# Reordering the products of a Strassen–Winograd step where a new token half enters the down projection (decoder block, eight cores)

## The chip, the cores and the metric

The kernel runs on one Trainium2 chip, on all 8 cores of it, one batch element per core. The metric is the device time in microseconds (us) of the slowest core. Most executions agree within 0.3%, but a program on eight cores also has a slower state, in which the cores of one die run at a lower granted clock.

## The reference, cut to what matters

A decoder block in two parts: token mixing (attention and mLSTM head groups), then a gated MLP with a causal three-tap convolution. The change touches the last line alone, the multiplication by `w_down`, and how the kernel passes into it.

```python
D_MODEL = 2048; BATCH = 8; SEQ = 2048; D_FF = 5632; FFN_CONV = 3
...
        h2 = _rmsnorm(x, norm_ffn_g[layer]).astype(x.dtype)
        u = _causal_dwconv(h2 @ w_up[layer], ffn_conv_w[layer], ffn_conv_b[layer])
        gate, val = jnp.split(u, 2, axis=-1)
        x = x + (jax.nn.silu(gate) * val) @ w_down[layer]
```

## The kernel before

Both MLP multiplications use the Winograd form of Strassen's method: seven products of half blocks in place of eight, paid for with sums of activations and of weights on the vector engine. The down stage has 16 steps, called d0 to d15: eight groups of output columns for the first 1024 tokens, then the same eight for the second 1024. A step computes four tiles of the output (x11, x12, x21, x22: token quarter, column block), from

- activations A11, A12, A21, A22 (token quarter, inner half). The up stage writes them to DRAM (`actd`); for d0, and again for d8, they are read back in eight loads of 1280 KB. S1 = A21 + A22, S2 = S1 − A11, S3 = A11 − A21, S4 = A12 − S2 are made on the vector engine in halves of 5120 elements;
- weights B11, B12, B21, B22 (640 KB each, loaded new for each step by the pool queue, as bf16) and T1 = B12 − B11, T2 = B22 − T1, T3 = B22 − B12 (written over B12), T4 = B21 − T2;
- a remainder: 20 of 22 chunk pairs of the inner dimension go through Winograd, the last two through "plain" products with their own small tiles of activations (`pA`) and weights (`pB`).

The products are P1 = A11·B11, P2 = A12·B21, P3 = S4·B22, P4 = A22·T4, P5 = S1·T1, P6 = S2·T2, P7 = S3·T3, each of 20 matmuls (128x128 by 128x512); with 16 plain ones a step has 156. They accumulate in PSUM banks; `acc` adds a bank to a tile of the residual `x1`, and the last one stores the tile to `outT`. Activation loads, `x1` loads and output stores share the sync queue.

Which tiles a product and a sum need, and how a step's weights get loaded (cut; every `...` is a cut):

```python
        def load(self, nm):
            k = ("B11", "B12", "B21", "B22").index(nm)
            i = self.q[nm]
            K.dma(pool, qv[i], w_down[self.g, :, k * KQ * 128:(k + 1) * KQ * 128], B_q[i], True)
...
        def t_sum(self, which):
            q = self.q
            o_, a, b = {1: ("T1", "B12", "B11"), 2: ("T2", "B22", "T1"), 3: ("B12", "B22", "B12"),
                        4: ("T4", "B21", "T2")}[which]
            tt_op(qv[q[o_]], B_q[q[o_]], qv[q[a]], B_q[q[a]], qv[q[b]], B_q[q[b]], ALU.subtract)
...
        def P1(self):
            self.p(self.s, "A11", "B11", True)
        def P5(self):
            self.p(2 + self.s, "S1", "T1", True)
        def P6(self):
            self.p(self.s, "S2", "T2", False)
        def P2(self):
            self.p(4 + self.s, "A12", "B21", True)
        def P7(self):
            self.p(self.s, "S3", "B12", False)
        def P4(self):
            self.p(self.s, "A22", "T4", False)
        def P3(self):
            self.p(2 + self.s, "S4", "B22", False)
```

What follows a product in program order: the load of the next step's tile into the buffer just read.

```python
    def aft(d, k):
        nx = downs[d + 1] if d + 1 < ND else None
        ...
        sw = nx.pr != downs[d].pr
        if sw:
            if k in (1, 5, 6, 2):
                a_load(*{1: ("A11", 1, "A11"), 5: ("S1", 1, "A12"), 6: ("S2", 1, "A21"), 2: ("A12", 1, "A22")}[k])
        elif k in (1, 5, 6, 2):
            nx.load({1: "B11", 5: "B12", 6: "B22", 2: "B21"}[k])
            if k == 2:
                nx.load_p()
        if k in (5, 2, 7, 4):
            nx.xload({5: "x11", 2: "x22", 7: "x12", 4: "x21"}[k])
```

The last up step's weight loads, and d0 (`gl` is the last up step, `g` is d0):

```python
        if n == len(ups) - 1:
            for i, nm in ((4, "B21"), (2, None), (3, "B22")):
                q_make(i)
                if nm:
                    d0.load(nm)
            d0.t_sum(1)
...
    a_make("A22")
    a_load("A22", 0, "A22")
    gl.P4()
    gl.taps(0)
    gl.P3()
    ...
    g.P1()
    acc(g, "x11", "A")
    aft(0, 1)
    g.P2()
    a_sum("S1", "A21", "A22", ALU.add)
    d0.t_sum(2)
    a_sum("S2", "S1", "A11", ALU.subtract)
    g.P5()
    d0.t_sum(3)
    d0.t_sum(4)
    a_sum("A21", "A11", "A21", ALU.subtract)
    acc(g, "x22", "B")
    g.P6()
    ...
    g.P7()
    ...
    plain_load(0)
    ...
    g.P4()
    g.P3()
    downs[1].t_sum(1)
    for nm, b in (("x12", "B"), ("x11", "C"), ("x21", "A"), ("x22", "D")):
        g.plain(nm)
        acc(g, nm, b, True)
    aft(0, 7)
    aft(0, 4)
    for k in (2, 3, 4):
        downs[1].t_sum(k)
```

The softmax here doesn't subtract the row's maximum and nothing guards it: scores larger than these inputs give would overflow.

## Time and profile before

| quantity | before |
|---|---|
| time, median of the first 3 runs | 2900.98 us (2900.79 to 2904.68) |
| span of the profiled run's slowest core (core 1) | 2902.3 us |
| spans of its eight cores | 2886.4 to 2902.3 us |
| tensor engine busy, core 1 | 97% |
| time lost in the down stage, mean of cores / core 1 | 47.1 / 51.9 us |

The last row is the measure called the **excess**. On each core it is the time from the start of the last up step's P4 (the first matmul after a gap of 0.84 us) to the end of the last matmul, less 2512 matmuls at 0.2158 us, 542.1 us. It counts waits and half clock together; half clock means stretches in which the tensor engine is granted 0.50 of its clock. In a timeline line the columns are start, length, engine, source line, operation, number of instructions, and in brackets the idle time just before and what ended it; L1262 is the down stage's matmuls, L1055 every bf16 sum, L1448 (L1450 after the change) the accumulations into `x1`, and L1286 and L1290 belong to the up stage.

### The profile page before, as it was taken

Reading aid. Unit: us, or ns where it says so; the run is one execution under the profiler, and the core shown is the slowest. Engines: PE = TensorE matmul, PEld = TensorE weight load, DVE = VectorE, ACT = ScalarE, POOL = GpSimd, SP = SyncE. Lnnn points to the kernel's source line nnn. Section 1 sums busy time; section 2 is a strip of 40 time slices with the busy share of each in tenths; the row PEclk is TensorE's granted clock in tenths of the full one; section 3 lists DMA queues with packets and bytes.
Section 4 is the critical chain, followed back from the end, with each engine's and each line's share of the span. In section 5 each row is a group of like instructions: output and inputs, shape, how many; then the busy total and the mean of one; then the engine's idle time right before and its main releaser. Section 6 shows DMA issues by size and latency. Waiting matters only on the chain.

```text
span 2902.3 us, 44182 instructions; the slowest of 8 cores (2886.4 to 2902.3 us)
## 1 busy us (share of the span) xinstructions
PE 2805.5 (97%) x14698; PEld 1333.3 (46%) x14698; DVE 1801.4 (62%) x2409; ACT 1222.3 (42%) x2013; POOL 369.1 (13%) x535
## 2 busy tenths in 40 slices
PE   6999999999999999999999999999999979997999
PEld 3444554555555544444444444444444434443444
DVE  4664543777777646688877777777788753324332
ACT  3567654666666521145555555555555400000000
POOL 0000001333333200011100000000011100000000
PEclk9999999999999999999999999999999989998999
DMA  8352455434444695757733333333368867787774
GB/s 201 94 82 51 78 113 119 92 85 88 90 88 87 132 250 179 181 87 105 106 66 66 66 66 66 66 66 66 66 99 148 206 140 152 145 220 151 144 150 93
DMA packets 223230, 330.23 MB, mean 114 GB/s; under 512 B 27008, under 2 KB 144192, under 8 KB 220960
## 3 DMA queue, kind: packets, MB, share of 16 engines
q0 software_dynamic: 98064, 156.79, 36.5%
q1 hardware_dynamic: 124944, 170.63, 20.2%
q8 instruction: 121, 1.98, 0.3%
q14 instruction: 101, 0.83, 0.1%
HBM read 386.30 MB, written 71.20 MB: 158 GB/s over the span
## 4 chain that ended last, share of the span: by engine, by line
PE 83%; DMA 6%; DVE 5%; issue 3%; ACT 2%; DVEq 0%; SPq 0%; POOL 0%; ACTq 0%; POOLq 0%
PE ps L1262 52%; PE ps L812 10%; PE ps L562 6%; PE ps L1136 4%; PE ps L433 3%; DMA mem<-xA 2%; DMA mem<-actd 2%; PE ps L911 2%; PE ps L913 1%; PE ps L898 1%; PE ps L421 1%; PE ps L836 1%; DVE mem L403 1%; DMA outT<-mem 1%; DVE mem L1055 1%
## 5 line engine op out<-in xcount | busy, mean ns | idle before, releaser
L1262 PE MATMUL ps<-mem 128*128 128x512 bf16 x7424 | 1617.2, 381 | 48.2 <-DMA mem<-actd 21.6
L1262 PEld LDWEIGHTS ps<-mem 128*128 128x128 bf16 x7424 | 727.9, 98 | 937.8 <-issue 72.7
L1320 DVE SCALAR_TENSOR_TENSOR mem<-mem,cfs 128x1024 f32<-128x1024 f32 x352 | 452.2, 1285 | 240.1 <-ACT mem L1314 154.6
L812 PE MATMUL ps<-mem 128*128 128x512 bf16 x1536 | 381.5, 379 | 0.0
L1055 DVE TENSOR_TENSOR mem<-mem 128x1024 bf16<-128x1024 bf16 (+3 forms) x324 | 308.6, 979 | 74.9 <-DMA mem<-w_down 58.3
L1448 DVE TENSOR_TENSOR mem<-ps,mem 128x512 f32<-128x512 f32 x128 | 88.2, 691 | 299.3 <-PE ps L1262 295.1
L166 POOL DMA_DIRECT2D mem<-w_up x240 | 126.9, 530 | 1145.3 <-PE ps L1262 744.7
L562 PE MATMUL ps<-mem 128*128 128x512 bf16 x1024 | 229.9, 380 | 0.0
L1136 PE MATMUL ps<-mem 128*128 128x512 bf16 x1024 | 224.9, 381 | 4.3 <-DMA mem<-mixd 3.5
L1286 ACT ACTIVATE mem<-ps 128x512 f32<-128x512 f32 x176 | 105.0, 597 | 288.8 <-PE ps L1262 288.6
L1314 ACT ACTIVATE mem<-mem,cfs 128x1024 f32<-128x1024 f32 x176 | 216.9, 1232 | 17.5 <-DVE mem L1290 10.7
L812 PEld LDWEIGHTS ps<-mem 128*128 128x128 bf16 x1536 | 148.6, 98 | 156.2 <-issue 8.0
L823 DVE SCALAR_TENSOR_TENSOR mem<-ps,cfs,mem 128x512 bf16<-128x512 f32 x192 | 143.9, 750 | 53.4 <-ACT mem L821 39.9
L1136 PEld LDWEIGHTS ps<-mem 128*128 128x128 bf16 x1024 | 100.3, 98 | 125.7 <-issue 8.2
L900 ACT ACTIVATE mem<-ps 128x512 bf16<-128x512 f32 x216 | 126.0, 583 | 70.8 <-PE ps L898 61.7
L832 POOL TENSOR_TENSOR mem<-mem 128x512 f32<-128x512 f32 x96 | 111.1, 1158 | 320.2 <-DMA mem<-mem 237.4
L901 DVE TENSOR_TENSOR mem<-mem 128x512 bf16<-128x512 bf16 x216 | 104.4, 484 | 75.7 <-ACT mem L900 75.3
L562 PEld LDWEIGHTS ps<-mem 128*128 128x128 bf16 x1024 | 99.1, 98 | 112.3 <-issue 1.4
L1290 DVE TENSOR_TENSOR mem<-ps,mem 128x512 f32<-128x512 f32 x176 | 120.4, 684 | 0.8 <-ACT mem L1286 0.7
L1159 ACT ACTIVATE mem<-mem 128x512 f32<-128x512 f32 x64 | 40.2, 629 | 169.7 <-DVE mem L1154 169.7
L433 PE MATMUL ps<-mem 128*128 128x512 bf16 x512 | 111.5, 379 | 0.0
L166 POOL DMA_DIRECT2D mem<-w_down x75 | 39.6, 531 | 535.0 <-PE ps L1262 434.2
(127 smaller groups left out, 2351.9 us busy)
## 6 DMA issues: line engine op xcount, KB each, us to landing
mem<-w_up POOLq DMA_DIRECT2D x240, 256.0 KB, 5.4
mem<-w_down POOLq DMA_DIRECT2D x60, 640.0 KB, 8.9
actd<-mem SPq DMA_DIRECT2D x88, 256.0 KB, 4.4
mem<-actd SPq DMA_DIRECT2D x16, 1280.0 KB, 13.0
mem<-xA SPq DMA_DIRECT2D x32, 512.0 KB, 10.7
mem<-xA SPq DMA_DIRECT2D x64, 256.0 KB, 6.1
x1d<-mem SPq DMA_DIRECT2D x64, 256.0 KB, 5.4
mem<-x1d SPq DMA_DIRECT2D x64, 256.0 KB, 5.3
```

Source lines behind the costliest of these rows:

```text
L166: eng.e.dma_start(out=o_, in_=i_).then_inc(sb.dsem, 16)
L433: bk, B_bk = dense(5, [lambda e, b, kc=kc: e.matmul(b[:], sl[:, kc, hm * 128:(hm + 1) * 128], hT[:, kc, tsl], start=(kc == 0), stop=(kc == ...
L562: ins = pe.e.matmul(ps[bi][:], *lr(kc), start=(kc == 0), stop=(kc == KC - 1))
L812: ins = pe.e.matmul(bank[:], sl[:, kc, c0:c0 + 128], hT[:, kc, tsl], start=(kc == 0), stop=(kc == KC - 1))
L823: K.op(dve, lambda e: e.scalar_tensor_tensor(out=sc[nm], in0=bank[:], scalar=cf[:, gcol:gcol + 1], in1=tab[:, tsl], op0=ALU.mult, op1=ALU. ...
L900: K.op(act, lambda e: e.activation(out=pt[:, c0:TT], in_=Sb[:, c0:TT], func=AF.Exp), [B_S], [B_p])
L1055: K.op(dve, lambda e: e.tensor_tensor(out=out, in0=a, in1=b, op=op), [B_a, B_b], [B_out])
L1136: ins = pe.e.matmul(ps[bi][:], wo_v[jb][:, kc, (jc % 4) * 128:(jc % 4 + 1) * 128], mix(T, kc), start=(kc == 0), stop=(kc == KC - 1))
L1262: K.mm([lambda e, l=l, r=r, s_=(first and i == 0): e.matmul(ps[bi][:], l, r, start=s_, stop=False, skip_group_check=True) for i, (l, r) in ...
L1290: K.op(dve, lambda e: e.tensor_tensor(out=y, in0=ps[bank][:], in1=snap[si], op=ALU.add), [B_ps[bank], B_snap[si]], [self.B_y[gv]])
L1314: K.op(act, lambda e: e.activation(out=self.a[gv], in_=self.y[gv][:, 2:1026], func=AF.Identity, scale=self.wc(gv, 2), bias=cf[:, CF_FCB + ...
L1320: K.op(dve, lambda e, k=k: e.scalar_tensor_tensor(out=self.a[gv], in0=self.y[gv][:, k:k + 1024], scalar=self.wc(gv, k), in1=self.a[gv], op ...
```

## The change

The intent: at d0 and d8, run products for which the data are there early, so that the tensor engine need not wait for the last activations and the sums made of them. P7 (which needs S3 = A11 − A21 alone) and P4 (which takes A22 as it comes) move ahead of P5 and P6, with banks of their own. For that S3 gets its own tile and is made in the up stage; T4, and with it T2, come earlier, so B22 is loaded before B21; the first half of A22 is loaded after the last up P6; each quarter of the plain activations gets a buffer record of its own, so their loads no longer wait for each other. The core of the diff (buffer addresses, the bodies of loads by halves and the d8 sums cut):

```diff
-    d_q = [dict(B11=1, B12=0, B22=3, B21=4, T1=2, T2=5, T4=2, spare=7)]
+    d_q = [dict(B11=1, B12=0, B22=4, B21=3, T1=2, T2=5, T4=1, spare=7)]
...
-        def P7(self):
-            self.p(self.s, "S3", "B12", False)
+        def P7(self, own=None):
+            self.p(self.s if own is None else own, "S3", "B12", own is not None)
...
+        if n == len(ups) - 1:
+            q_make(4)
+            d0.load("B22")
+            a_make("S3", [0])
+            a_sum("S3", "A11", "A21", ALU.subtract, [0])
...
         g.P6()
+        if n == len(ups) - 1:
+            a_make("A22", [0])
+            a_load("A22", 0, "A22", [0])
...
         if n == len(ups) - 1:
-            for i, nm in ((4, "B21"), (2, None), (3, "B22")):
-                q_make(i)
-                if nm:
-                    d0.load(nm)
+            q_make(3)
+            d0.load("B21")
+            q_make(2)
             d0.t_sum(1)
+            a_make("S3", [1])
+            a_sum("S3", "A11", "A21", ALU.subtract, [1])
...
     gl.P4()
-    gl.taps(0)
+    a_make("A22", [1])
+    a_load("A22", 0, "A22", [1])
     gl.P3()
...
-    g.P1()
-    acc(g, "x11", "A")
-    aft(0, 1)
-    g.P2()
-    a_sum("S1", "A21", "A22", ALU.add)
-    d0.t_sum(2)
-    a_sum("S2", "S1", "A11", ALU.subtract)
-    g.P5()
...
+    d0.t_sum(2)
+    g.P1()
+    d0.t_sum(4)
+    a_sum("A21", "A21", "A22", ALU.add)
+    acc(g, "x11", "A")
+    g.P2()
+    g.P7(7)
+    a_sum("S2", "A21", "A11", ALU.subtract)
+    g.P4(1)
...
+    aft(0, 1)
+    aft(0, 5)
+    g.P5()
+    acc(g, "x22", "B")
+    aft(0, 2)
+    a_make("S4")
+    a_sum("S4", "A12", "S2", ALU.subtract)
+    g.P6()
+    mid(g)
+    aft(0, 6)
     g.P3()
     downs[1].t_sum(1)
-    for nm, b in (("x12", "B"), ("x11", "C"), ("x21", "A"), ("x22", "D")):
-        g.plain(nm)
-        acc(g, nm, b, True)
+    plains(g)
     aft(0, 7)
     aft(0, 4)
     for k in (2, 3, 4):
         downs[1].t_sum(k)
...
         if d == NG:
+            a_sum("S4", "A11", "S2", ALU.subtract)
+            acc(g, "x11", "A")
+            aft(d, 1)
             g.P2()
-            ...
+            aft(d, 2)
+            ...
+            g.P7(7)
+            ...
+            g.P4(1)
             g.P5()
             acc(g, "x22", "B")
             aft(d, 5)
+            ...
             g.P6()
+            mid(g)
             aft(d, 6)
             g.P3()
+            nx.t_sum(1)
+            plains(g)
```

## The prediction

> **What bounds the kernel now.** I read the page's engine shares and slices first, then who the tensor engine waits for, then its timeline around the two dips that the slices show, and last the vector engine and the DMA queues in those two stretches.
>
> ```profile
> PE 2805.5 (97%) x14698; PEld 1333.3 (46%) x14698; DVE 1801.4 (62%) x2409; ACT 1222.3 (42%) x2013; POOL 369.1 (13%) x535
> ...
> PE   6999999999999999999999999999999979997999
> ...
> DVE  4664543777777646688877777777788753324332
> ...
> PEclk9999999999999999999999999999999989998999
> ```
>
> The matmul stream is the bound: 97% busy. A slice is 72.6 us, and in the down stage only slices 33 and 37 fall to 7: the start of each half of the down stage, where the activations of a new token half come in (call its steps d0 and d8; there are 16 steps, d0 to d15, of 7 x 20 + 16 = 156 matmuls). What those two cost, on the slowest core, by waits and then in order of time:
>
> ```profile
> PE ps L1262 <- DMA mem<-actd: 21.6, 3, 16.8
> ...
> PE ps L1262 <- DVE mem L1055: 11.0, 6, 4.4
> PE ps L1262 <- DVE mem L1448: 7.9, 2, 7.0
> ```
>
> ```profile
> 2303.61 12.25 PE L1262 MATMUL ps<-mem 128*128 128x512 bf16 x56 [0.84 <-ACT mem L1286]
> 2318.34 2.32 PE L1262 MATMUL ps<-mem 128*128 128x512 bf16 x10 [2.49 <-DVE mem L1055]
> 2325.07 9.39 PE L1262 MATMUL ps<-mem 128*128 128x512 bf16 x30 [4.40 <-DVE mem L1055]
> 2341.41 5.91 PE L1262 MATMUL ps<-mem 128*128 128x512 bf16 x20 [6.95 <-DVE mem L1448]
> ...
> 2360.19 2.42 PE L1262 MATMUL ps<-mem 128*128 128x512 bf16 x8 [3.13 <-DMA mem<-actd]
> ...
> 2613.99 2.32 PE L1262 MATMUL ps<-mem 128*128 128x512 bf16 x10 [1.60 <-DVE mem L1055]
> ...
> 2642.61 254.96 PE L1262 MATMUL ps<-mem 128*128 128x512 bf16 x1168 [16.84 <-DMA mem<-actd]
> ```
>
> At d0 the third product needs S1, which needs the last quarter of the activations (A22), loaded only after the last up product; then the vector engine makes every other sum in one run of eight, and an accumulation queued behind them frees the bank for the next product (the 6.95 us):
>
> ```profile
> 2315.37 2.83 DVE L1055 TENSOR_TENSOR mem<-mem 128x5120 bf16<-128x5120 bf16 x1 [2.96 <-DMA mem<-actd]
> 2322.09 17.97 DVE L1055 TENSOR_TENSOR mem<-mem 128x5120 bf16<-128x5120 bf16 x8 [3.90 <-DMA mem<-actd]
> 2339.99 1.28 DVE L1448 TENSOR_TENSOR mem<-ps,mem 128x512 f32<-128x512 f32 x2
> ```
>
> At d8 the big wait is for the small "plain" activations, the last 2 of 22 chunk pairs. The sync queue issues them late, and one after the other:
>
> ```profile
> SPq L60 <- DMA outT<-mem: 46.5, 17, 21.1
> SPq L60 <- DMA mem<-actd: 31.5, 4, 15.1
> ```
>
> The clock pays once more after the long wait, which the timeline books as busy time (columns after the stretch: its length, busy time of PE, PEld, DVE, ACT, POOL, granted clock, DMA):
>
> ```profile
> 2642.60:2645.00 2.40, 2.40 (x6) 0.85 (x7) 0.07 (x1) 0.00 (x0) 0.00 (x0) 0.50 0.31 80
> 2645.00:2650.00 5.00, 5.00 (x17) 1.92 (x16) 0.62 (x1) 0.00 (x0) 0.00 (x0) 0.69 0.69 227
> ```
>
> **The loss in numbers.** A warm product of 8 matmuls takes 1.727 us (an up step of 7 is 12.085 us apart from the next), so one matmul costs 0.2158 us. From the end of the 0.84 us gap to the end are 2 x 8 + 16 x 156 = 2512 matmuls, 542.1 us. Core 1 takes from 2303.61 to 2642.61 + 254.96 = 2897.57, 593.96 us: 51.9 us too long. The waits in the timeline explain 40.5 of them, half clock after them the rest: step d1 begins at 2367.9 (its third accumulation at 2376.87 less 0.3 and two products of 4.32), so d0 lost 27 us; d9 begins at 2661.8, so d8 lost 24.5. The same sum for cores 0 to 7 gives 45.3, 51.9, 44.8, 49.3, 44.3, 45.8, 48.7 and 46.8 us. This is the ceiling of the change. Core 2 enters the stage last (2304.58, core 1 at 2303.61), so it may end last when both lose alike.
>
> **What the Trainium skill says.** "TensorE: Matmul & The Clock Gate", Part 1: the array falls to half clock after an idle window of some 3.4 us and needs about as long a busy one to come back; warm N=512 matmuls start every 215.7 ns. The trace agrees: 0.50 then 0.69 after the 16.84 us wait, and 215.8 ns. So gaps over 3.4 us cost more than themselves, and small ones do not. "VectorE: DVE Perf Modes", Side-by-side: a 16-bit tensor_tensor makes two elements a cycle, plus about 150 cycles; for 5120 that is an estimate of 2.83 us, and the trace has 2.82; so these sums get no cheaper and the change can only reorder them. "DMA: Bandwidth & Descriptors", Queues, rings and completion order: each DMA engine takes turns between queues, and starts a queue's own transfers in order. The trace fits: three output stores issued at 2597.8 behind eight activation loads landed after 22.3 us (2.9 is their median); a weight load that shared the engines with A22 took 12.8 us, alone 7.0 to 8.8. "SBUF — State Buffer", Who interferes with whom: tensor_tensor has no two-port mode, so a busy vector engine should not starve the pool queue's descriptor writing. No long bf16 run in this trace tests that.
>
> **The change, part by part.** The matmuls stay the same in kind and number. In d0 and d8 the products go P1 P2 P7 P4 P5 P6 P3 in place of P1 P2 P5 P6 first. P7 needs only S3 (A11 - A21), P4 only A22 as it comes. Both get own banks, 7 and 1, so nothing in a bank has to be read out before them; for that bank 0 and bank 7 are added by 5 accumulations in place of 2: 3 more per step, 6 x 0.69 = 4.1 us of vector time. S3 gets its own tile and is made while the up stage still runs. Half of A22 loads after the last P6 (about 2299), not after the last P7 (2306); the other half after P4. B22 now comes before B21. The plain tiles get one buffer per half, so their loads no longer wait for each other.
>
> *d0, vector engine as the clock of it.* From the last but one up step, with 2.75 us for a half sum (back to back), 1.43 for a weight sum, 0.6 for an accumulation, 2.6 for two taps: S3 first half 2299.5 to 2302.3, taps 2304.9, up sum 2305.5, product 2306.6, T1 2308.1, S3 second half 2310.8, up sum 2311.4, T3 2312.9, four taps 2318.1, product 2319.2, T2 2320.7, T4 2322.1, S1 2327.6, accumulation 2328.2, S2 2333.7, accumulation 2334.3, S4 2339.8, five accumulations 2343.1, next T1 2344.5, accumulation 2345.2. The tensor engine: P3 of the last up step starts 0.4 late, P1 to 2311.9, P2 2316.2, P7 2320.5 (S3 and T3 are ready), P4 waits 2 for T4, to 2326.6; P5 2330.9; P6 waits 0.7 for S2, to 2336.0; P3 waits 1.8 for S4, to 2342.1; plains 2345.6. Ideal is 2340.7: 4.9 us lost in waits too short to cool the clock. One thing more: T3 needs B22, second in the pool queue at about 2297.8 and sharing with A22. At the weights' rate alone and beside loads (0.65 MB in 12.8 us) I put it at 2311 to 2314, so add 1.5. d0 loses 6.4 in place of 27.
>
> *d8.* S3's source A21 lands at 2602 and about 2606 (issued 2581.2, 20.6 us), so S3 is ready at 2609.3 for P7 at 2612.2. A22 lands at 2611 and 2615, P4 wants it at 2616.5; S1 is ready at 2617.8, P5 wants it at 2620.8. S2 and S4 follow by 2631.7, P3 needs its second half at 2631.6. The sync queue stays stuck behind the output store until 2620.9, but then issues all four plain loads within 2 us: landing 2629 to 2632, wanted at 2633.8. The last bank of d8 is freed after T1 of d9, which needs a weight load issued after P5 (2625.1 + 10 = 2635): d9 starts near 2639 in place of 2637.3. d8 loses about 2 in place of 24.5.
>
> Sum: 6.4 + 2 = 8.4, say 9 lost. Core 2 then ends at 2304.6 + 542.1 + 9 + 4.7 (last matmul to end, as core 1 has it) = 2860.4 against 2902.3 now: 42 us less. From 2900.98 that is 2859; I say 2860.
>
> **The rivals.** *The vector engine is the bound of d0.* It is in my sum; its queue is in order and full from 2299 to 2345, so each microsecond of late B22, B21 or A22 goes straight through. If B22 lands at 2317 the gain falls by 5: 2865. *Loads collide.* Three weights and A22 within 10 us; the slices show the engines full there already. If in d8 the plain loads, still behind the stores, take the 15.4 us that the first of them takes now, the tensor engine waits 3 to 5 us there and may cool: 2866 to 2870. Against it: the weights that they share with now (three issued at 2626.3) are partly spread to earlier and later. *Only the listed waits go, the cold clock stays*: 2870; it would need gaps above 3.4 us to remain. *All goes*: 51.9 away would be 2850. A loss needs a new stall of over 40 us; no order of buffers that I find has one.
>
> **Range and chances.** Some four fifths of the ceiling with some 5 us of doubt for each of two steps gives 2850 to 2871. Faster by 2% means under 2843, below the ceiling of any core: 0.02. Slower by 2%: 0.02.
>
> **What would show it.** Right: the waits for actd nearly gone, the 16.84 and 6.95 us gaps gone, d0 with waits of 1 to 3 us on L1055 sums before P4, P6 and P3, and the clock at 1.00 in both steps; vector busy time up by 4 us. Wrong: a wait of the vector engine on w_down before T3 of over 3 us, a tensor wait on actd at the plains of d8, or steps d1 to d7 and d9 to d15 longer than 33.7 us.

## The result

| | before | after |
|---|---|---|
| median of all runs | 2904.68 us of 15 | 2879.41 us of 13 |
| fast runs | from 2900.16 us | 2876.18 to 2890.09 us |
| ratio of fast runs, 95% interval | | 0.992, 0.9909 to 0.9932 |
| excess, mean of cores / largest, profiled run | 47.1 / 51.9 us | 20.4 / 31.2 us |
| spans of the cores, profiled run | 2886.4 to 2902.3 us | 2848.1 to 2876.9 us |

A ratio here and below is the mean time of one kernel's fast runs over the mean of the other's fast runs of the same rounds, so it is not quite the ratio of the medians quoted. Executions in which one die ran at a lower clock are left out of the means. The changed kernel is 0.8% faster: within 2%, as predicted, but the gain is some 23 us where 41 were predicted, and 2879 lies outside the range of 2850 to 2871.

The page of the changed kernel, which belongs to core 7, its slowest; two of the rows that the prediction shows of before:

```profile
PE 2800.3 (97%) x14698; PEld 1332.5 (46%) x14698; DVE 1802.3 (63%) x2415; ACT 1222.6 (42%) x2013; POOL 369.1 (13%) x535
...
PE   6999999999999999999999999999999979998999
```

The tensor engine has as many matmuls and the vector engine six more instructions, as worked out. Slice 37 (d8) has risen from 7 to 8, slice 33 (d0) still reads 7. Who the tensor engine of core 7 waited for, in the view of waits:

```profile
PE ps L1262 <- DMA mem<-w_down: 8.2, 1, 8.2
PE ps L1262 <- DMA mem<-actd: 7.9, 1, 7.9
PE ps L1262 <- DVE mem L1450: 7.5, 3, 6.0
```

The 6.95 us on an accumulation and the waits for the sums of S1 are gone, the 16.84 us on the plain activations has become 7.88, and two waits are new. The first of the lines did not exist before at all. The tensor engine's timeline of core 7 shows where they are:

```profile
2298.86 1.89 PE L1262 MATMUL ps<-mem 128*128 128x512 bf16 x8 [0.84 <-ACT mem L1286]
2300.91 6.20 PE L1262 MATMUL ps<-mem 128*128 128x512 bf16 x28 [0.17 <-DVE mem L1290]
2315.31 31.68 PE L1262 MATMUL ps<-mem 128*128 128x512 bf16 x136 [8.19 <-DMA mem<-w_down]
2347.87 8.79 PE L1262 MATMUL ps<-mem 128*128 128x512 bf16 x40 [0.88 <-DVE mem L1450]
2362.62 257.51 PE L1262 MATMUL ps<-mem 128*128 128x512 bf16 x1182 [5.96 <-DVE mem L1450]
...
2630.68 4.94 PE L1262 MATMUL ps<-mem 128*128 128x512 bf16 x16 [7.88 <-DMA mem<-actd]
```

Count the matmuls. After the 0.84 us gap come 8 and 28: P4 and P3 of the last up step (16) and the 20 of P1 of d0. So the 8.19 us wait stands before **P2 of d0**, and what P2 reads is A12, long there, and B21. The 5.96 us wait comes 40 matmuls into d1, after its P1 and P5: it is before P6 of d1, which needs the bank that the accumulation of P1 frees. The 7.88 us wait stands before the plain products of d8.

In numbers for core 7: d0 should have taken 172 matmuls, to 2335.98; d1 starts at 2347.87, so 11.9 us went in d0 (the wait of 8.19, short ones of 0.17 and 0.88, and half clock: 136 matmuls took 31.68 us, 2.3 more than at full clock). The wait in d1 costs 6.1, half clock behind it 2.4 (1182 matmuls in 257.51 us in place of 255.08), d8 costs 10.6. The sum is 31.0 of the 31.2 us. The prediction had 6.4 for d0, nothing for d1 and 2 for d8, rounded up to 9.

Why P2 waits: B21 is now third in the pool queue behind B12 and B22, and three loads that were issued over 12 us before (at 2296.7, 2298.3 and 2308.6 on core 1) are now issued within 1.3 us, with the first half of A22 among them. On core 7 B12, B22 and B21 were issued at 2293.9, 2294.5 and 2295.2 and landed after 8.2, 16.7 and 19.9 us; on core 1 before, the order was B12, B21, B22, after 7.0, 8.8 and 12.8. The DMA views of a stretch of 60 us around d0, of before on core 1 and of after on core 7 (size of one transfer, median us from issue to landing):

```profile
mem<-w_down POOLq DMA_DIRECT2D x7, 640.0 KB, 8.8
mem<-actd SPq DMA_DIRECT2D x2, 1280.0 KB, 12.0
```

```profile
mem<-w_down POOLq DMA_DIRECT2D x7, 640.0 KB, 16.7
mem<-actd SPq DMA_DIRECT2D x2, 1280.0 KB, 17.1
```

The same seven weights take nearly twice as long. The windows view says that the DMA engines became busy nearly all the time: the last two columns are their busy share and GB/s, over 55 us from 5 us before the last up step's P4, first before on core 1, then after on core 7 (columns as in the prediction):

```profile
2298.60:2353.60 55.00, 39.38 (x161) 16.10 (x160) 42.45 (x29) 7.78 (x9) 3.95 (x8) 0.88 0.68 153
```

```profile
2293.90:2348.90 55.00, 44.91 (x197) 19.13 (x195) 47.53 (x36) 7.89 (x9) 4.76 (x9) 0.91 0.94 186
```

The tensor engine runs 197 matmuls in place of 161 in that time, so the loads that its products release come closer together, and they are busy for 0.94 of the stretch in place of 0.68. The vector engine's timeline of core 7 shows what that does in d0 and d1:

```profile
2311.43 1.49 DVE L1055 TENSOR_TENSOR mem<-mem 128x2560 bf16<-128x2560 bf16 x1 [4.24 <-DMA mem<-w_down]
...
2357.57 4.30 DVE L1055 TENSOR_TENSOR mem<-mem 128x2560 bf16<-128x2560 bf16 x3 [8.06 <-DMA mem<-w_down]
2361.79 1.28 DVE L1450 TENSOR_TENSOR mem<-ps,mem 128x512 f32<-128x512 f32 x2
```

The first line is T3 of d0 waiting 4.24 us for B22. The second is T2 to T4 of d1: they stand in program order before d1's accumulations, and wait 8.06 us for B22 of d1, the last of five weight loads issued from 2331.0 to 2339.6, which took 17.8 us. The third is the two accumulations behind them; the first ends at 2362.5, and P6 of d1 starts at 2362.62.

At d8 the sync queue is the place to look. Its timeline on core 7:

```profile
2586.11 1.98 SPq L166 DMA_DIRECT2D outT<-mem  x3
2615.01 0.33 SPq L166 DMA_DIRECT2D mem<-x1d  x1
...
2617.09 2.31 SPq L166 DMA_DIRECT2D mem<-actd  x4
```

Three output stores are issued behind eight activation loads; the queue then stands until they land (the next `x1` tile goes into their buffer), and the plain activations come only after that, at 2617.1. d8 started at about 2592, so the queue moved again 23 us after the step's start; before, that was 17.3 us. The stores took 27.7 us; on core 1 before, 22.3. This differs by core: before, they took 21.5 to 23.9 us (medians) on all eight; now they take 11.0 to 19.8 us on five cores and 27.7 to 29.6 us on cores 1, 4 and 7, and these three are the cores that wait at the plain products of d8 (7.0 to 7.9 us). B21 and pB of the next step, now released early by P2, run beside the stores; experiment 5 tests what that does. The four plain loads are indeed issued within 2.3 us of each other, as predicted, and land after some 11.6.

Last, the cores differ: the excess of cores 0 to 7 is 14.0, 26.0, 14.5, 9.1, 27.3, 22.4, 18.7 and 31.2 us. Core 3 has the 9 that was predicted for all. Cores 0 and 6 also wait where core 7 does not, 5.21 and 1.67 us for the plain activations of d0. The slowest core decides the time.

### The profile page after: what moved, and what is told of

Read it like the earlier page. It is cut to its first block, busy times and chain, and to the rows that moved or that the text cites. A ratio compares the mean times of both kernels' runs of the same rounds, so it can differ in the third digit from the quotient of the medians.

```text
span 2876.9 us, 44190 instructions; the slowest of 8 cores (2848.1 to 2876.9 us)
## 1 busy us (share of the span) xinstructions
PE 2800.3 (97%) x14698; PEld 1332.5 (46%) x14698; DVE 1802.3 (63%) x2415; ACT 1222.6 (42%) x2013; POOL 369.1 (13%) x535
## 4 chain that ended last, share of the span: by engine, by line
PE 83%; DMA 6%; DVE 4%; issue 3%; ACT 2%; SPq 0%; DVEq 0%; POOL 0%; ACTq 0%; POOLq 0%
PE ps L1262 52%; PE ps L812 11%; PE ps L562 6%; PE ps L1136 3%; PE ps L433 3%; DMA mem<-xA 2%; PE ps L911 2%; PE ps L913 2%; PE ps L898 1%; DMA mem<-w_down 1%; PE ps L836 1%; PE ps L421 1%; DMA outT<-mem 1%; DVE mem L403 1%; DVE mem L1154 1%
## 5 line engine op out<-in xcount | busy, mean ns | idle before, releaser
L1366 DVE TENSOR_TENSOR mem<-mem 128x1024 bf16<-128x1024 f32 x88 | 106.9, 1215 | 0.2 <-DVE mem L1320 0.2
```

## The experiments

Each is an edit of the changed kernel. Two theories run through them. **Q**: the place of a transfer in program and queue order decides; give the late tile another place and the time falls by its wait. **H**: the bytes of the stretch bind; a tile made earlier makes another one late, and only fewer bytes help. Other letters stand in the expectations that use them; there e2, e4, e10 and e11 are experiments 2, 3, 5 and 6. All ratios are against the kernel before on the same chip: experiments 1 to 4 ran on one chip, 5 to 9 on a second, 10 on a third. On the second, one fast run of the kernel before took 2923.5 us, which widens the intervals.

Excess and waits are those of one profiled execution, and executions of one kernel differ: the changed kernel had a mean excess of 20.4 us, and 22.3 in a second execution. In kernels whose edit lies elsewhere, the mean wait over the cores is 4.3 to 4.9 us before P2 of d0, 2.2 to 3.8 before P6 of d1, and 2.6 to 5.4 for activations in d8. Only what leaves these ranges is taken as an effect.

**1. B21 before B22 in the last up step.**

```diff
         if n == len(ups) - 1:
+            q_make(3)
+            d0.load("B21")
             q_make(4)
             d0.load("B22")
 ...
-            q_make(3)
-            d0.load("B21")
```

> Edit: in the last up step B21 is loaded before B22 instead of after it; nothing else. Theory Q (three weights land one after the other in the pool queue, and the vector engine's chain is hung on T3, which needs B22): P2's wait for its weights falls from 2.7-8.2 us to under 4.5 us per core, but T3 starts some 3-4 us later, P7 or P4 then wait for the vector engine instead, and the time is 0 to 4 us longer than the changed kernel (2877 to 2883; ratio to before 0.992-0.994). Rival N (the wait of P2 is the loss, and goes when its weights come earlier): 3 to 6 us shorter, ratio 0.990.

Measured: ratio 0.9929 (0.9911 to 0.9946), median of the fast runs 2877.7 us; excess 18.6 mean, 24.7 at most. The wait of P2 on the weights falls from 4.8 us (mean of cores) to 0.8, so the place of B21 makes that wait. But the time stays, as the expectation had it, and its rival N fell: T2 and T4 now come late, and the cores wait 6.2 us for sums in d0. Core 6's timeline, P2 first and then P4:

```profile
2314.17 4.48 PE L1262 MATMUL ps<-mem 128*128 128x512 bf16 x20 [1.58 <-DMA mem<-w_down]
...
2330.42 16.91 PE L1262 MATMUL ps<-mem 128*128 128x512 bf16 x69 [5.53 <-DVE mem L1055]
```

The wait has moved from one weight to the other: in the terms above, the first point for H.

**2. The first half of A22 loaded with the second, after the last up P4.**

```diff
         g.P6()
-        if n == len(ups) - 1:
-            a_make("A22", [0])
-            a_load("A22", 0, "A22", [0])
 ...
-    a_make("A22", [1])
-    a_load("A22", 0, "A22", [1])
+    a_make("A22")
+    a_load("A22", 0, "A22")
```

> Edit: the first half of A22 is again loaded with the second, after P4 of the last up step, instead of 8 us earlier. Theory Q (the early A22 load takes engine time from the three weights, which are wanted sooner): B22 lands about 4 us earlier (no wait of the vector engine before T3), P2's wait falls to 0-3 us, A22 is still in time for P4; mean loss over the cores falls by 3-5 us, time 2874 (ratio 0.990-0.991). Rival R (a weight takes its 8-9 us whatever else runs, only its place in the queue counts): P2's wait stays at 2.7-8.2 us, time unchanged or 1-3 us longer because A22 comes later.

Measured: ratio 0.9925 (0.9911 to 0.9938), fast median 2878.1 us; excess 21.8 / 28.7. The wait of P2 falls to 1.05 us in the mean, without any reordering of weights: the half of A22 running beside them makes B21 late too, and either edit is enough to remove most of the wait. The gain is given back one step later: on core 2, whose d0 has no wait above 1.2 us, P6 of d1 waits for its accumulation,

```profile
2362.79 3.57 PE L1262 MATMUL ps<-mem 128*128 128x512 bf16 x8 [9.87 <-DVE mem L1450]
```

and over the cores that wait is 5.2 us where it was 3.7. The expectation held for the wait and failed for the time.

**3. In d0, the next step's B21 and plain weights loaded after B22.**

```diff
-    aft(0, 2)
     a_make("S4")
 ...
     aft(0, 6)
+    aft(0, 2)
```

> Edit: for step d1 the weight B22 is asked for before B21 and the small plain weights, instead of after them. Theory Q (in d1 the vector engine stands before T2 of d1 until B22 has come, and the accumulation that frees the bank for P6 is queued behind it): the wait of the vector engine for w_down there falls from 3.7-8.1 us to under 2, P6 of d1 waits under 1 us instead of 1.5-6 us; mean loss 3-4 us smaller, time 2873-2875 (0.9905). Rival H (the bytes in flight bound it, their order does not matter): the wait moves to B21, P2 of d1 waits instead, time unchanged.

Measured: ratio 0.992 (0.9908 to 0.9933), fast median 2877.9 us; excess 20.2 / 29.8. The waits for accumulations before P6 and P7 of d1 fall from 3.7 to 1.3 us, as they should if B22's place made them. The time does not follow: in d1 the vector engine now waits 4 to 16 us for an `x1` tile on seven cores (5 to 7 on four cores before this edit), whose load is released later too, and d8 waited 5.4 us in this execution. A miss on the time; H has the time right, but named B21 as the next to wait for.

**4. The eight big activation loads of d8 on the scalar engine's queue.** If the sync queue's order holds the stores back, this frees them.

```diff
+        q = act if pr else sp
 ...
-            sp.wait(t)
+            q.wait(t)
 ...
-            K.dma(sp, v.rearrange("p (k t) -> p k t", t=TT), ...
+            K.dma(q, v.rearrange("p (k t) -> p k t", t=TT), ...
```

> Edit: the eight large activation loads for d8 go through the scalar engine's DMA queue, idle in this stage, instead of the sync queue. Theory Q (the sync queue stands behind output stores, and these behind 10.5 MB of loads in the same queue): the stores that now land after 12-30 us land in under 8, the plain loads are issued some 10-20 us earlier, the 5-8 us waits for actd before the plains of d8 go on all cores; excess of the worst core falls from 31 to 20-23 us, time 2868-2871 (ratio 0.988-0.989). Rival H (the DMA engines are full for those 30 us and only total bytes count): the waits move to A21 and A22 (S3, S1), time within 3 us of the changed kernel.

Measured: ratio 0.9923 (0.9908 to 0.9938), fast median 2878.5 us; excess 22.0 / 27.8. The stores land after 9.7 to 13.9 us over the cores in place of 11.0 to 29.6 (on core 2 after 13.9 in place of 15.8); Q had expected under 8. But what shares the engines with them gets slower in turn: the vector engine's waits on core 2 in d8 now hold

```profile
DVE mem L1055 <- DMA mem<-actd: 11.4, 3, 6.4
```

which this core does not have in the changed kernel, and the tensor engine's waits in d8 are 2.4 us on activations and 2.2 on accumulations (mean of cores) where they were 3.0 and 1.1. Queue order is real, but with its gain another transfer pays: Q falls for the time, H stands.

**5. In d8, the next step's B21 and plain weights loaded after P6, not after P2.**

```diff
             g.P2()
-            aft(d, 2)
 ...
             aft(d, 6)
+            aft(d, 2)
```

> Edit: in d8 the loads of B21 and of the small plain weights for d9 are asked for after B22, about 17 us later, as before the change; only their place moves. Theory Q (these 0.9 MB now run beside the held-up output stores and hold up the plain activations behind them): the stores land 4-6 us sooner in d8, the 5-9 us waits for actd before the plains fall to 0-4 us, mean excess falls by 2-3 us, time 2870-2875 (ratio 0.990-0.991). Rival H (what the stretch d7-d8 has to move is too much for its time, whatever the order): the wait moves to the last accumulation of d8 or to B21 in d9, time within 2 us of the changed kernel.

Measured: ratio 0.9896 (0.9847 to 0.9946), three fast runs 2874.11 to 2877.56 us; excess 18.8 / 27.6. The waits for activations in d8 fall from 3.0 to 0.3 us in the mean, and those at the plain products go on all cores. The three stores land after 14.2 to 24.8 us over the cores in place of 11.0 to 29.6 (on core 7 after 24.8 in place of 27.7), in one execution each. What is added is a wait of the last bank of d8: the vector engine waits 4.9 us for a weight of d9 on core 7, and the accumulations cost 2.5 us in the mean where they cost 1.1. The median, 2874.92 us, is some 4 us below that of the changed kernel's runs and inside what Q expected; three fast runs are too few to tell it from them, so here Q is not refuted.

**6. Experiments 2, 3 and 5 together**, run on two occasions.

> Three edits together: first half of A22 late (as e2), B22 of d1 ahead of B21 (as e4), B21 of d9 late (as e10). Theory Q (the e2 gain of 3.8 us in d0 was given back in d1 because B22 of d1 comes when it comes; with e4's order it is kept): mean excess 11-14 us in place of 20, worst core 18-20, time 2866-2869 (0.988). Rival H: one of the three stretches takes the loss back, mean excess 18-21, time 2875-2879.

Measured: ratio 0.9921 (0.9866 to 0.9977); three of its fast runs lie at 2871.8 to 2874.2 us, one at 2907.7. Excess 10.8 / 18.7 in the profiled run. Because of the one long run it was taken again beside the changed kernel:

> The three edits of e11 once more (its first timing was spoilt by slow states). Theory Q: mean excess 10-12, worst core 15-19, 2866-2870, ratio 0.988-0.9895, 9-11 us under the changed kernel on the same chip. Rival H: 2875-2879, ratio 0.991-0.993.

Measured: ratio 0.9897 (0.987 to 0.9925), median 2874.42 us of six fast runs (2871.46 to 2878.9); excess 16.9 / 32.5: on core 4 the accumulation before P7 of d1 was waited for 9.8 us. Q's time is missed on both occasions; its excess was met in the first execution (10.8) and not in the second, so an excess of one execution is good to some 6 us here and no better.

> The changed kernel again, unedited, as the measure for the two others on the same chip. Both theories: mean excess 19-22, worst core 26-32, ratio to before 0.991-0.993.

Measured, on the same chip: ratio 0.9911 (0.9877 to 0.9945), median 2878.92 us, fast runs 2875.89 to 2881.25; excess 22.3 / 28.6. So the three edits together are worth some 4 us, and this is the best correct version found; the intervals against the kernel before overlap.

**7. The activation loads of d8 halved** (the other half of each tile keeps old data). Its output is wrong, which doesn't matter for the time.

```diff
+            m = 5 if pr else 10
-            K.dma(sp, v..., actd[pr, th, kp, :, i * 10:(i + 1) * 10, :], B, True)
+            K.dma(sp, v[:, :m * TT]..., actd[pr, th, kp, :, i * 10:i * 10 + m, :], B, True)
```

> Wrong results on purpose: the eight large activation loads for d8 bring only half their bytes (5.2 MB less); nothing else. Rival H and Q both say that d8's waits fall; they differ in what is left: if the bytes of the stretch are the bound (H), actd waits in d8 go to 0 on all cores and d8 keeps under 1 us of waits; if the place of the small loads behind the stores were enough (Q), stores would still land after 10 us and 1-3 us remain on the cores that wait now. Mean excess falls by 4-5 us, time 2868-2872 (0.9885-0.990), d0 and d1 as in the changed kernel.

Measured: ratio 0.9879 (0.9829 to 0.9929), two fast runs 2867.39 and 2871.35 us; excess 13.6 / 15.6. On all cores the only wait left in d8 is one of 0.36 us. Core 1's timeline through d8:

```profile
2579.64 40.09 PE L1262 MATMUL ps<-mem 128*128 128x512 bf16 x185
2620.08 20.27 PE L1262 MATMUL ps<-mem 128*128 128x512 bf16 x93 [0.35 <-DVE mem L1055]
```

Every instruction, order and queue is as in the changed kernel; only bytes are fewer, as H expected. The stores now land after 2.1 to 3.5 us on all cores, where Q expected over 10. The packets do not become fewer (on core 1, 3691 in 82 us on the sync queue in the changed kernel, 4309 in 80 us here), only smaller, so it is bytes and not packets. Fewer bytes also shorten the queue in front of the stores, so this run alone does not part H from Q; experiment 4, which freed the queue and left the bytes, does. Together they say: in d8 the bytes bind.

**8. The plain activations in one buffer record per token quarter again**, to see what that part of the change is worth.

```diff
-        pA[i], B_pA[i] = mview(lo, 2048, BF16), [K.mbuf("pA%d_%d" % (i, kp), lo + kp * 2048, lo + kp * 2048 + 2048)
-                                                 for kp in range(2)]
+        pA[i], B_pA[i] = mview(lo, 2048, BF16), [K.mbuf("pA%d" % i, lo, lo + 4096)] * 2
```

> Edit: the plain activation tiles get one buffer per token half again, so the second load of each waits for the first; undoes one part of the change. Theory Q: the waits before the plains of d8 grow by 3-5 us on all cores (the second loads of a pair are issued one landing later), and d0's plains stay without a wait as their loads have 15 us to spare; time 2880-2884 (0.993). Rival: the engines are full there, so the pieces land at the same time as before and nothing changes.

Measured: one fast run of four, 2884.45 us, and no ratio; excess 23.1 / 31.6, d8 waits 4.4 us on activations. The changed kernel had 3.0 in one execution and 4.55 in the other. Inconclusive. That the plain products of d0 have time to spare is wrong, here (9.4 and 7.2 us on cores 5 and 6) as in the changed kernel.

**9. Experiment 6, and T3 and T4 of d1 and d9 behind the first two accumulations.**

```diff
-    for k in (2, 3, 4):
-        downs[1].t_sum(k)
+    downs[1].t_sum(2)
 ...
         aft(d, 5)
+        if d in (1, NG + 1):
+            g.t_sum(3)
+            g.t_sum(4)
```

> e11 and one edit more: in d1 and d9 the vector engine makes T3 and T4 after the accumulations that follow P1 and P5, not before, so a late B21 no longer holds up the bank that P6 needs. Theory Q: the waits of P6 in d1 on an accumulation (0 to 4.3 us by core in e11) fall under 1 us, mean excess 8-9.5, worst core 12-15, 2862-2867, ratio 0.987-0.988. Rival V (T2 itself comes too late, the order of the vector engine is no matter): the waits move from the accumulation to the sum and stay, time as e11.

Measured: ratio 0.9896 (0.9856 to 0.9936), three fast runs 2871.95 to 2875.95 us; excess 13.2 / 25.8. No better than experiment 6. The accumulations of d1 are still waited for, 4.6 us in the mean and up to 10.6; but now the vector engine waits not for a weight but for an `x1` tile. Core 0's vector engine, and its sync queue:

```profile
2375.91 0.69 DVE L1450 TENSOR_TENSOR mem<-ps,mem 128x512 f32<-128x512 f32 x1 [17.43 <-DMA mem<-x1d]
```

```profile
2345.30 4.52 SPq L166 DMA_DIRECT2D outT<-mem  x4
2365.74 6.74 SPq L166 DMA_DIRECT2D mem<-x1d  x4
```

The `x1` loads are issued 20 us after the stores whose buffers they take. The expectation missed: the next transfer in line became the bound.

**10. Fewer bytes in all three places** (half of each weight of d0 and d1 except B12 of d1, half of A22 of d0, half of d8's activations). Its output is wrong, which doesn't matter for the time. Order, queues, sums and products are untouched, so this asks whether the prediction's timetable of the vector engine was right.

```diff
+            m = 5 if pr or src == 'A22' else 10
-            K.dma(sp, v..., actd[pr, th, kp, :, i * 10:(i + 1) * 10, :], B, True)
+            K.dma(sp, v[:, :m * TT]..., actd[pr, th, kp, :, i * 10:i * 10 + m, :], B, True)
 ...
+            m = KQ * 64 if self.d < 2 and (self.d, nm) != (1, "B12") else KQ * 128
-            K.dma(pool, qv[i], w_down[self.g, :, k * KQ * 128:(k + 1) * KQ * 128], B_q[i], True)
+            K.dma(pool, qv[i][:, :m], w_down[self.g, :, k * KQ * 128:k * KQ * 128 + m], B_q[i], True)
```

> Wrong results on purpose: the changed kernel with half the bytes in the weight loads of d0 and d1 (one of the eight kept whole), in A22 of d0 and in the eight activation loads of d8; order of instructions and buffers untouched. If transfers that come late are the whole of what the prediction missed (theory Q and H alike), the vector engine's timetable of the prediction stands alone: no waits for w_down or actd, P4 of d0 waits about 2 us for T4, d0 loses 4-6, d1 under 1, d8 under 1; mean excess 6-8 us, worst core under 11, 2857-2862, ratio 0.985-0.9865. Rival V (the vector engine's chain is longer than the timetable says): mean excess 11-16 with waits on sums and accumulations.

Measured: ratio 0.9863 (0.984 to 0.9887), fast runs 2857.35 to 2864.45 us; excess **6.2 us on every one of the eight cores**. Core 3's timeline (the accumulations are L1452 in this kernel):

```profile
2312.36 14.84 PE L1262 MATMUL ps<-mem 128*128 128x512 bf16 x68 [0.17 <-DVE mem L1290]
2329.48 16.97 PE L1262 MATMUL ps<-mem 128*128 128x512 bf16 x70 [2.28 <-DVE mem L1055]
...
2352.87 263.91 PE L1262 MATMUL ps<-mem 128*128 128x512 bf16 x1222 [0.23 <-DVE mem L1452]
```

P2 and P7 follow P1 without a gap, P4 waits 2.28 us for T4, and after d0 one stretch of 1222 matmuls runs without a wait. d1 starts at 2352.87, 5.4 us later than 172 matmuls after 2310.30, where the prediction had 4.9 with the data there in time; d8 costs 0.6 where it had 2. So with the data there in time the order of the change loses what the prediction said, and no more; the spread between cores is gone as well.

One thing is not as predicted: the 70 matmuls after the 2.28 us took 1.7 us more than at full clock. The first 3 us after that same wait, on core 3 and on core 6 (the third column from the end is the granted clock):

```profile
2329.48:2332.48 3.00, 3.00 (x10) 1.24 (x11) 3.00 (x2) 0.00 (x0) 0.00 (x0) 0.67 0.80 235
```

```profile
2314.18:2317.18 3.00, 3.00 (x14) 1.36 (x15) 3.00 (x2) 0.00 (x0) 0.00 (x0) 1.00 0.82 210
```

On six cores the clock fell to 0.50 for some 3 us, on cores 4 and 6 not at all. Those two wait 1.0 us more before P3 instead: the vector engine sets the pace of d0, and all eight come to 6.2. The 14 us from the mean of 20.4, and the 25 us from the largest of 31.2, are transfers.

## Why the prediction was wrong

- **What bounded the kernel before, and the ceiling: right.** The waits and the half clock behind them were read correctly, and core 1's 51.9 us of excess was the sum to win. Of the waits named, those of 6.95 us and for S1 are gone, the 16.84 us is gone on five cores and 7.0 to 7.9 us on three, and the plain activations of d0 are still waited for on two.
- **The vector engine's timetable of d0: right.** 4.9 us predicted (6.4 with a late B22), with 2 for P4 waiting for T4; experiment 10 has 5.4 on core 3 and 2.28 there on all cores.
- **"Gaps over 3.4 us cost more than themselves, and small ones do not": wrong, and harmless by luck.** The prediction drew this from the idle window of some 3.4 us in Part 1 of "TensorE: Matmul & The Clock Gate". Here waits of 2.28 us were followed by a clock of 0.50 on six of eight cores (experiment 10), one of 2.42 us already on core 3 of the kernel before; one of 3.26 us (changed kernel, core 0) and one of 3.84 us (experiment 6, second occasion, core 4) left it at 1.00. So the length of a wait alone does not decide, and no rule comes out of these runs. It cost nothing in d0 because the vector engine set the pace there.
- **"P1 to 2311.9, P2 2316.2": this is the step that failed.** It let P2 follow P1 without asking for B21, which P2 reads and which the change moved behind B22; B21's landing has no place in the working; it is named only in the first rival, as a load whose lateness the vector engine would pass on. Measured, P2 waits 4.8 us in the mean and 8.2 on core 7, and cools the clock there. Experiments 1 and 2 remove that wait, in two ways.
- **The 1.5 us added for B22 was mis-sized** by the same error, a transfer time taken from a trace in which fewer loads ran at once: T3 waited 4.24 us on core 7. A weight load took 16.7 us (median around d0) where the trace before had 8.8, and 12.8 beside A22, which the prediction used.
- **The timetable ended at d0's last accumulation.** "Next T1 2344.5, accumulation 2345.2" is followed by T2 of d1, and nothing asked when its B22 lands: 6.1 us and 2.4 of half clock on core 7. The prediction named "steps d1 to d7 longer than 33.7" as what would show it wrong, and d1 is such a step; its two other signs, a wait of over 3 us for `w_down` before T3 and a wait for `actd` at the plain products of d8, came too. In the sum "6.4 + 2 = 8.4, say 9" the terms measured on core 7 are 11.9 for d0, 8.5 for d1, which has no term, and 10.6 for d8.
- **d8: the mechanism was right, its size was not.** The queue was taken to be stuck as long as before, 17.3 us from the step's start; on core 7 it was 23. B21 and pB, which the new order releases earlier, are part of that (experiment 5); why the stores took longer on three cores and less on five stays open. 10.6 us lost on core 7 for 2 predicted. The rival "loads collide" named this, with a wait of 3 to 5 us and half clock; it saw the three weights and A22 of d0 too, but put a cost on d8 alone, and its outcome at 2866 to 2870. It should have been the main line and counted for all three places.
- **One figure for all cores.** Before, the excess differed by 8 us over the cores; after, by 22. On core 3 the prediction was met (9.1). The mean of the cores' spans is 2866.6 us in ten fast runs, the slowest core's mean is 2878.6. The guess that the core entering the stage last ends last fell too: in the profiled run core 7 entered at 2298.86, with core 2 at 2305.09, and ended last, because it lost most. On core 7 the sum reads 2298.9 + 542.1 + 31.2 + 4.7 = 2876.9; predicted was 2304.6 + 542.1 + 9 + 4.7.

- **"No long bf16 run in this trace tests that": one does.** During the run of eight sums that the prediction shows (2322.09, 17.97 us) the pool queue issued a weight load at 2335.2 on core 1. It landed after 5.8 us, the shortest of all weight loads there, so this long run of sums did not hold it up.

What is shown: the waits that are gone or shorter, the three that cost core 7 its time and their places, that each of them goes or shrinks when its own transfer is moved, that all but some 4 us is then lost elsewhere, and that all of them go when the bytes are fewer. What stays open: why cores of one execution, which run the same program, see loads of such different speed (below); why engines that are busy for 0.94 of a stretch move 186 GB/s in it, where slices of 1.5 us of it reach 370; and what the splitting of the plain buffers alone is worth.

## What to carry to other kernels

When a change lets the tensor engine run sooner, it also pulls the loads that its products release closer together: take the transfer times from the stretch as it will be, by bytes over time, not from a trace in which those loads ran apart, and follow every operand of every product to its landing, the moved loads first. Carry the timetable one step beyond the place that was changed, since a late tile is paid for at whatever waits behind it in an in-order queue. If moving a late transfer removes its wait and not the time, test with fewer bytes before trying another order.

## What the Trainium skill lacked or had wrong

- "DMA: Bandwidth & Descriptors", Anatomy of one DMA, fits a transfer with 2.0 us plus bytes over 436 GB/s; for 640 KB as landed that is an estimate of 3.5 us. The weight loads, which cast while they load, took 5.8 us at best on core 1 before, 8.8 in the median around d0, and 16.7 there on core 7 after the change. The page gives no rate for a casting load, nor a figure for how the time grows when two queues share the engines; the prediction would have needed just that. Its section Queues, rings and completion order lets each engine take turns between queues and start a queue's transfers in order. The runs agree (stores behind eight loads landed after 21.5 to 23.9 us before the change and 11.0 to 29.6 after, and after 9.7 to 13.9 with the loads on another queue), but no figure there says what this costs the issuing engine: on core 7 a wait for such a store held every later load of the sync queue back until 23 us into d8.
- "TensorE: Matmul & The Clock Gate", Part 1, expects 13/16 of the clock once three cores of a die run dense matmuls. Here all eight did, and the fast runs of the changed kernel were granted 0.990 to 0.998 of it in the mean on every core; only in slow runs did one die fall, for instance to 0.84 to 0.85 (the run of 3309.6 us). So the lower clock is a state of some executions here and not the rule. The same part's idle window of some 3.4 us did not decide here when the clock fell (2.28 us was enough on six cores, 3.84 us was not on another).
- How evenly two neighbouring cores get on in one execution: no page gives a figure for it. In ten fast runs of the changed kernel the spans of neighbouring cores (0 and 1, 2 and 3, 4 and 5, 6 and 7) differ by 15.0 us in the mean, those of other pairs by 10.7: where one of two neighbours is quick, the other tends to be slow. The kernel before has it too (11.4 and 8.5 in six fast runs), and so has experiment 10 (9.5 and 6.7 in four), whose down stage cost every core the same in the profiled execution; so not all of it arises in the down stage. No run here shows why.
